# Tuned float32 transformer block: a new order of the first token tiles, the first column group's product in true float32, and a new entry to the second SwiGLU

## The chip, the cores and the metric

The kernel runs on one core of a Trainium2 chip, in one launch. The metric is the device time of that launch in microseconds (us); what counts is the median of several runs.

## The reference

One block on x of 1024 tokens by 1024 channels, all in float32: a SwiGLU of half weight, a mix of two attentions, and a second SwiGLU of half weight.

```python
def rms_norm(x, g):
    x32 = x.astype(jnp.float32)
    y = x32 * lax.rsqrt(jnp.mean(x32 * x32, axis=-1, keepdims=True) + EPS) * g.astype(jnp.float32)
    return y.astype(x.dtype)

def swiglu(h, w_in, w_out):
    gate, up = jnp.split(h @ w_in, 2, axis=-1)
    return (jax.nn.silu(gate) * up) @ w_out

def hybrid_layer(x, ...):
    x = x + 0.5 * swiglu(rms_norm(x, ffn1_norm), ffn1_w_in, ffn1_w_out)
    h = rms_norm(x, mix_norm)
    proj = h @ w_mix_in
...
    x = x + mix @ w_mix_out
    x = x + 0.5 * swiglu(rms_norm(x, ffn2_norm), ffn2_w_in, ffn2_w_out)
    return x
```

The inner width of a SwiGLU is 2816, that is 22 column groups of 128 for the gate and as many for the other half. The change touches only the start of each SwiGLU; the attention between them is left as it is.

## The kernel before

**Tiles and products.** The tokens lie in eight tiles of 128, `X[0]` to `X[7]`; in instruction names these are `x_74` to `x_81`, and the trace calls all of them `x`. Each tile has two halves of 512 channels (`HALF`). A tile is scaled by its inverse root mean square, transposed on TensorE (`flip4`, L312, four 128x128 float32 transposes for a half), and copied back from PSUM in place (L552 on VectorE, which multiplies by the norm's gain on the way where one is given; L557 on ScalarE where none is). Products need float32 accuracy and use the float32r type: both operands are split into a high part and a low part, and a product is three matmuls, high by high, low by high, high by low (`mm3`, L250 to L252). The high part of a transposed half comes from ScalarE (L540) or GpSimd (L545), the low part from VectorE (L320, `flip_lo`). Weights are split in the same way by `split` (high L456 or L458, low L461).

**The order.** All steps are entered into a list scheduler with `add(engine, cost, position, emit, deps, after, takes, tail)`; it writes out, for each engine, one fixed order by the costs and positions given. Engines run that order in sequence and wait on semaphores, so an instruction that waits holds up all behind it on its engine. Loads and stores are issued by SyncE, in the order of the list too.

**The start of a SwiGLU** (`first_stage`). The tokens are taken in two sets, tiles 0 to 3 and 4 to 7 (`half` 0 and 1), so that a product has 512 columns. The first two column groups (`plain=2`) are plain products, group 0 and group 1 for either set; the other groups save products by working on sums and differences of halves (`S1` to `S4`, made by L704). The four weight blocks of a group (two halves of channels, gate and other) are 256 KB each.

**At the start of the kernel** a tile's two halves are loaded one by one, squared on ScalarE (L501), and the inverse root is a square root on ScalarE (L507) with a Newton step on VectorE (L474 to L477); L1004 scales the tile, half of tiles 0 and 1 on VectorE and the rest on GpSimd, which also splits all four weight blocks of group 0 into high and low (L458, L461). TensorE runs `WARM` = 8 groups of three warm-up transposes first (L489). Group 0 for tiles 0 to 3 is computed in two pieces of 256 columns (`pieces`), all else in 512.

**At the end of the attention** the block's last products (`pvo`, L1889 and L1890, with the low parts `pl` from VectorE, L1880) are followed by the last output products (`mo`, L250 to L252). Between them tiles 0 to 3 enter the second SwiGLU: the gain of its norm is loaded into `Psel` (4 KB, to all partitions), L521 multiplies a tile by its inverse root and by the gain in one VectorE operation of 128x1024, tile 3 takes two GpSimd operations for each half (L2011, L2013); then come the transposes, the copy back on ScalarE, high parts on GpSimd and low parts on VectorE.

Of the kernel before, what the change touches and what calls it, by code (L numbers as in the profile page):

```python
# [8 lines left out]
F32 = mybir.dt.float32  # L9
# [10 lines left out]
NT = 8  # L20
D = 1024
# [167 lines left out]
def block_kernel(  # L189
# [248 lines left out]
    def fetch(src, pos, deps=(), k=4, tail=2.2, cost=0.75):  # L438

        b, us = {}, []  # L440

        def emit():
            b["r"] = ws.place()
            dma(b["r"].rearrange("p (k f) -> p k f", k=k) if k > 1 else b["r"], src)
        fetched.append(add("S", cost, pos, emit, deps=deps, after=fetched[-1:], takes=[(r_raw, us)], tail=tail))
        return b, fetched[-1], us
# [33 lines left out]
    def root(st, pos, dep, table=0.0):  # L480
        c = add("A", 0.1 + table, pos, lambda: ACT.activation(st["y"], st["v"], AF.Sqrt), deps=[dep])
# [55 lines left out]
    def split_half(place, dst, t, pos, deps, eng="A"):  # L537

        def high():
            (ACT.activation if eng == "A" else copy_pool)(dst()[0][:, :, t % 4 * 128:t % 4 * 128 + 128], place(), AF.Copy)  # L540
        hi = add(eng, 0.6, pos, high, deps=deps)
        return [hi, add("D", 0.69, pos, lambda: flip_lo(place(), dst(), t), deps=[hi])]

    def copy_pool(o, i, _):
        POOL.tensor_scalar(o, i, 1.0, 1.0, op0=OP.mult, op1=OP.mult)  # L545

    def flip_in_place(t, c, dst, pos, deps, free, gain=None):
# [3 lines left out]
        if gain:  # L551
            back = add("D", 0.69, pos, lambda: DVE.tensor_tensor(  # L552
                in_blocks(t, c), b["p"].rearrange("p (k t) -> p k t", k=4),
                gain(c).unsqueeze(2).to_broadcast([128, 4, 128]), op=OP.mult), deps=[p])
            au.append(back)
            return [back] + split_half(lambda: in_blocks(t, c), dst, t, pos, [back, *free])
        back = add("A", 0.6, pos, lambda: ACT.activation(  # L557
            in_blocks(t, c), b["p"].rearrange("p (k t) -> p k t", k=4), AF.Copy), deps=[p])
        au.append(back)
        return [back] + split_half(lambda: in_blocks(t, c), dst, t, pos, [back, *free], "G" if t < 4 else "A")  # L560
# [39 lines left out]
    def open_in(p, x):  # L600
# [1480 lines left out]
```

## Time and profile before

| | us |
|---|---|
| median of 3 runs | 1925.83 (1923.86 to 1927.3) |
| the profiled execution's own time | 1925.15 |
| its span in the trace | 1923.4 |
| TensorE busy | 1877.4 (98%) |
| VectorE busy | 1379.9 (72%) |
| ScalarE busy | 921.7 (48%) |
| GpSimd busy | 433.9 (23%) |

The span runs from the first to the last instruction of the profiled execution; its own time is 1.75 us longer, and the median of the runs lies 0.68 us above that. TensorE is busy nearly all the time, so a time can only be won where TensorE waits, or where it does less, or where its clock is low. In the profile's rows PE is TensorE, DVE VectorE, ACT ScalarE, POOL GpSimd, SP SyncE. "out<-in" names what an instruction writes and reads, x8 that eight of a kind are merged in a row, and brackets hold the idle time before a row and what ended it.

### The profile page before, as it was taken

Reading aid. Unit: us, or ns where it says so; the run is one execution under the profiler, and the core shown is the slowest. Engines: PE = TensorE matmul, PEld = TensorE weight load, DVE = VectorE, ACT = ScalarE, POOL = GpSimd, SP = SyncE. Lnnn points to the kernel's source line nnn. Section 1 sums busy time; section 2 is a strip of 40 time slices with the busy share of each in tenths; the row PEclk is TensorE's granted clock in tenths of the full one; section 3 lists DMA queues with packets and bytes.
Section 4 is the critical chain, followed back from the end, with each engine's and each line's share of the span. In section 5 each row is a group of like instructions: output and inputs, shape, how many; then the busy total and the mean of one; then the engine's idle time right before and its main releaser. Section 6 shows DMA issues by size and latency. Waiting matters only on the chain.

```text
span 1923.4 us, 27849 instructions
## 1 busy us (share of the span) xinstructions
PE 1877.4 (98%) x9014; PEld 1564.6 (81%) x9014; DVE 1379.9 (72%) x3119; ACT 921.7 (48%) x1955; POOL 433.9 (23%) x574
## 2 busy tenths in 40 slices
PE   7999999999999999998899999989999999999999
PEld 6788888888888888887788778777888888888887
DVE  7977876665655677567888888879878766655553
ACT  5433333334444444246877888745333333344442
POOL 5111111111000112014754765542111111110000
PEclk9999999999999999998999999999999999999999
DMA  5367753336986337244201321023676532368662
GB/s 170 103 229 237 233 187 100 99 121 224 310 274 190 103 97 193 66 133 157 67 19 61 97 69 56 23 77 98 230 241 227 189 104 91 128 226 307 192 217 99
DMA packets 244083, 290.76 MB, mean 151 GB/s; under 512 B 25169, under 2 KB 139233, under 8 KB 243937
## 3 DMA queue, kind: packets, MB, share of 16 engines
q1 hardware_dynamic: 243936, 288.98, 46.7%
q8 instruction: 71, 1.16, 0.3%
q14 instruction: 76, 0.61, 0.1%
HBM read 201.72 MB, written 90.33 MB: 152 GB/s over the span
## 4 chain that ended last, share of the span: by engine, by line
PE 92%; DVE 4%; ACT 2%; POOL 2%; issue 1%; DMA 1%; SPq 0%; DVEq 0%; ACTq 0%; POOLq 0%
PE lg L251 13%; PE lg L250 13%; PE lg L252 13%; PE mo L250 6%; PE mo L251 6%; PE mo L252 6%; PE pv L250 4%; PE pv L252 4%; PE pv L251 4%; PE ptr L1870 3%; PE a L250 3%; PE a L251 3%; PE a L252 3%; PE pvo L1890 2%; PE pvo L1889 2%; PE lg L1695 2%
## 5 line engine op out<-in xcount | busy, mean ns | idle before, releaser
L834 POOL TENSOR_TENSOR x<-x,x 128x512 f32<-128x512 f32 x80 | 116.5, 1456 | 684.6 <-DVE x L830 628.8
L461 DVE TENSOR_TENSOR wlo<-wraw,whi 128x512 fp32r<-128x512 f32 x286 | 207.7, 732 | 70.8 <-ACT whi L456 69.3
L456 ACT ACTIVATE whi<-wraw 128x512 fp32r<-128x512 f32 x274 | 170.3, 623 | 102.2 <-PE lg L251 46.0
L461 DVE TENSOR_TENSOR gpl<-graw,gph 128x512 fp32r<-128x512 f32 x154 | 106.8, 697 | 124.6 <-ACT gph L456 124.6
L456 ACT ACTIVATE gph<-graw 128x512 fp32r<-128x512 f32 x154 | 96.1, 629 | 190.6 <-PE pv L251 88.2
L826 ACT ACTIVATE x<-lg 128x512 f32<-128x512 f32 x96 | 57.4, 598 | 156.5 <-PE lg L252 156.4
L1880 DVE TENSOR_TENSOR pl<-ptr,ph 128x512 fp32r<-128x512 f32 x178 | 116.4, 684 | 17.4 <-ACT ph L1878 16.2
L1878 ACT ACTIVATE ph<-ptr 128x512 fp32r<-128x512 f32 x178 | 98.7, 595 | 33.1 <-PE ptr L1870 32.0
L88 POOL TENSOR_SCALAR whi<-wraw 128x512 fp32r<-128x512 f32 (+1 forms) x52 | 35.2, 681 | 320.1 <-PE mo L252 211.6
L456 ACT ACTIVATE whi<-x 128x512 fp32r<-128x512 f32 x108 | 67.4, 627 | 82.2 <-PE lg L251 41.6
L251 PE MATMUL lg<-xn0l,whi 128*128 128x512 f32 (+1 forms) x264 | 100.9, 382 | 3.3 <-DVE xn0l L320 3.3
L250 PE MATMUL lg<-xn0h,whi 128*128 128x512 f32 (+1 forms) x264 | 101.3, 384 | 3.0 <-ACT xn0h L540 1.5
L250 PE MATMUL a<-whi,gph 128*128 128x512 f32 x264 | 103.1, 391 | 0.0
L252 PE MATMUL a<-whi,gpl 128*128 128x512 f32 x264 | 102.8, 389 | 0.0
L251 PE MATMUL a<-wlo,gph 128*128 128x512 f32 x264 | 102.7, 389 | 0.0
L252 PE MATMUL lg<-xn0h,wlo 128*128 128x512 f32 (+1 forms) x264 | 100.5, 381 | 0.0
L461 DVE TENSOR_TENSOR wlo<-x,whi 128x512 fp32r<-128x512 f32 x108 | 73.7, 685 | 32.2 <-ACT whi L456 31.7
L830 DVE TENSOR_TENSOR x<-lg,x 128x512 f32<-128x512 f32 x72 | 49.7, 690 | 55.9 <-PE lg L252 55.4
L250 PE MATMUL lg<-whi,gph 128*128 128x512 f32 x198 | 77.0, 389 | 0.0
L252 PE MATMUL lg<-whi,gpl 128*128 128x512 f32 x198 | 77.0, 389 | 0.0
L251 PE MATMUL lg<-wlo,gph 128*128 128x512 f32 x198 | 77.0, 389 | 0.0
L1758 POOL TENSOR_SCALAR Psel<-Psel,sc,gates 128x256 f32<-128x256 f32 (+7 forms) x60 | 52.1, 871 | 45.8 <-DVE sc L1750 19.5
(518 smaller groups left out, 5684.6 us busy)
## 6 DMA issues: line engine op xcount, KB each, us to landing
wraw<-in_ffn_w_in_dram SPq DMA_DIRECT2D x176, 256.0 KB, 3.4
wraw<-in_ffn_w_out_dram SPq DMA_DIRECT2D x66, 256.0 KB, 3.3
x<-in_ffn_w_out_dram SPq DMA_DIRECT2D x44, 256.0 KB, 4.0
qd<-qst SPq DMA_DIRECT2D x32, 256.0 KB, 2.2
xn0l<-qd SPq DMA_DIRECT2D x32, 256.0 KB, 2.8
wraw<-in_w_mix_in_dram SPq DMA_DIRECT2D x28, 256.0 KB, 2.9
x<-in_x_dram SPq DMA_DIRECT2D x12, 512.0 KB, 7.8
side<-in_ffn_w_out_dram SPq DMA_DIRECT2D x22, 256.0 KB, 4.6
```

Of the source, the lines that this page charges most:

```text
L250: PE.matmul(o, ah, bh, start=first, stop=False, **kw)
L251: PE.matmul(o, ah, bl, start=False, stop=False, **kw)
L252: PE.matmul(o, al, bh, start=False, stop=last, **kw)
L456: ACT.activation(w["h"], b["r"], AF.Copy)
L461: low = add(low, 0.69 if low == "D" else 1.25, pos + 0.5, lambda e=DVE if low == "D" else POOL: e.tensor_tensor(w["l"], b["r"], w["h"].bit ...
L826: ACT.activation(b["r"], o["o"], act)
L830: return add("D", 0.69, at, lambda b=tb[k], o=bx[o]: DVE.tensor_tensor(b["r"], o["o"], b["r"], op=OP.add), deps=deps)
L834: return add("G", 1.25, at, lambda a=tb[a], b=tb[b]: POOL.tensor_tensor(a["r"], a["r"], b["r"], op=OP.mult), deps=deps)
L1758: POOL.tensor_scalar(P[:, off:e], P[:, off:e], sc, gate, op0=OP.mult, op1=OP.mult)
L1870: PE.transpose(p[:, h * 128:(h + 1) * 128], s.P[h][:, c:c + 128], ident)
L1878: ACT.activation(st["ph"], st["p"], AF.Copy)
L1880: lo = add("D", 0.6, pos + 0.2, lambda st=st: DVE.tensor_tensor(st["pl"], st["p"], st["ph"].bitcast(F32), op=OP.subtract), deps=[hi])
```

## The change

In the first SwiGLU:

1. Group 0 for tiles 0 to 3 is no longer made of split parts. `whole` multiplies the weights as loaded (`raw0`, float32) by the transposed tile in place (float32), one matmul of 128x128x128 for each of four blocks, two halves and two parts: 16 a tile, 64 in all, in place of 96 of 256 columns. `raw0` stands where the high part of `S2` comes later (`s2_place`).
2. The tiles come one by one: tile 0's transposes, its product, tile 1's transposes, its product, and so on. Inverse roots are made by `inv_rms_of`, for tiles 1 to 3 singly, for 4 and 5 and for 6 and 7 together. Scaling goes by halves (`scale_half`): VectorE and ScalarE for tiles 0 and 1, GpSimd for the rest.
3. The split of group 0 is due later, since only tiles 4 to 7 need it now; its low parts go to VectorE.
4. Tile 1's load waits for 1.7 us in the plan (`come(1.7)`), and the plan now puts two other loads ahead of it.
5. Group 0 for tiles 4 to 7 is computed in two pieces of 256 columns.

In the second SwiGLU: the gain is no longer loaded to all partitions and multiplied; `gcol2` holds it by channel, and the copy back multiplies it, on VectorE. Scaling goes by halves, ScalarE for the first half of tiles 0 to 3, GpSimd for all else. The transposes take first halves of tiles 0 to 3, then second halves; the second wait for tile 3's first (`fl["A11", 3]`). High parts go to ScalarE.

```diff
-    def scale_in_place(t, r, gain, pos, deps):
-        return add("D", 1.22, pos, lambda: DVE.scalar_tensor_tensor(
-            X[t], X[t], r(), gain(), op0=OP.mult, op1=OP.mult), deps=deps)
+    def scale_half(t, c, r, pos, deps, eng, **kw):
+        def emit():
+            x = X[t][:, HALF[c]]
+            if eng == "A":
+                ACT.activation(x, x, AF.Copy, scale=r())
+            elif eng == "D":
+                DVE.tensor_scalar(x, x, r(), None, op0=OP.mult)
+            else:
+                POOL.tensor_scalar(x, x, r(), 1.0, op0=OP.mult, op1=OP.mult)
+        return add(eng, {"A": 0.6, "D": 0.36, "G": 0.66}[eng], pos, emit, deps=deps, **kw)
+    def inv_rms_of(a, n, pos, deps):
...
+        for t in range(a, a + n):
+            for h in range(2):
+                sq.append(add("A", 0.75, pos, lambda t=t, h=h, first=not sq: (first and place(), square(t, h)), deps=deps[t - a],
+                              after=sq[-1:], takes=[] if sq else [(r_y, yu)]))
+        return st, root(st, pos, add("D", 0.4, pos, total, deps=sq), late=0.2)[1], yu
...
-            wait = fl["A11", 1] if begin and t < 2 and c else []
-            fl[name, q] = flip_in_place(t, c, lambda: opn()[name], at, deps + wait[-1:], free, gain)
+            wait = fl["A11", 3][-1:] if t < 4 and c and not begin else []
+            fl[name, q] = flip_in_place(t, c, lambda: opn()[name], at, deps + wait, free, gain, 6.0 if begin and t < 4 else 0.0)
...
+        def whole(o, raw, t, j):
+
+            x = in_blocks(t, j)
+            for a in range(4):
+                PE.matmul(o["o"][:, 128 * t:128 * t + 128], raw["r"][:, 128 * a:128 * a + 128], x[:, a], start=j == a == 0,
+                          stop=j == 1 and a == 3, skip_group_check=True)
...
-                    W[n, j, part] = split(b, t, us, pos - 4.0 + 8 * n, weigh, low="G" if begin and n == 0 else "D")
+                    W[n, j, part] = split(b, t, us, pos + (16.0, 6.0)[n] + 0.4 * j + 0.2 * part if begin else pos - 4.0 + 8 * n, weigh)
...
-                for c0, c1 in (pieces if n == half == 0 else [(0, 512)]):
+                for t, j, part in [(t, j, part) for t in range(4) for j in range(2) for part in range(2)] if begin and n == half == 0 else []:
...
+                    chain.append(add("P", 0.95, at, emit, deps=[arrived, here[0]], after=chain[-1:], takes=takes))
+                    at += 0.68
...
+                for c0, c1 in [] if begin and n == half == 0 else pieces if n == 0 else [(0, 512)]:
...
+            if begin and q == 0:
+                s2_open = [add(None, 0.0, at, begin, after=[u for j in range(2) for k in range(2) for u in raws[0, j, k][2]])]
+            parts_of("S2", q, t, 0, at + 2.0, [s2, opened], s2_open if begin else [])
...
-            fetched.append(add("S", 1.7, -20.0, lambda t=w_: load_x(t, n=2 if t < 4 else 1), after=fetched[-1:], tail=2.6))
+            fetched.append(add("S", 1.9, -20.0, lambda t=w_: load_x(t, n=2 if t < 4 else 1), after=fetched[-1:], tail=2.8,
+                               deps=[come(1.7)] if w_ == 1 else []))
...
-    gain2 = add("S", 1.5, tail, lambda: load_gain(nx["t"][:, 0, :D], ffn2_norm), deps=[nb], tail=2.2)
...
-        scaled[t] = scale_in_place(t, lambda t=t: R2[:, t:t + 1], lambda: nx["t"][:, 0, :D], p_, [put_, r_, gain2])
+        scaled[t] = [scale_half(t, c, lambda t=t: R2[:, t:t + 1], p_ + c, [put_, r_], "A" if t < 4 and c == 0 else "G") for c in range(2)]
```

How the order of instructions moves is shown at three places; `raw_401` is `raw0`.

TensorE at the kernel's start, before: after the warm-ups the first halves of tiles 0 and 1, then products of split parts (`xn0` from tiles, `whi` and `wlo` from weights) for both.

```order
L489 MATMUL warm<-ident 128x128 x24
L312 MATMUL ntr<-ident,x_74 128x128 x4
L312 MATMUL ntr<-ident,x_75 128x128 x4
L250 MATMUL lg<-xn0h,whi 128x256
L251 MATMUL lg<-xn0l,whi 128x256
L252 MATMUL lg<-xn0h,wlo 128x256
```

TensorE at the same place, changed, up to group 1's first product:

```order
L491 MATMUL warm<-ident 128x128 x24
L312 MATMUL ntr<-ident,x_74 128x128 x8
L671 MATMUL lg<-x_74,raw_401 128x128 x16
L312 MATMUL ntr<-ident,x_75 128x128 x8
L671 MATMUL lg<-x_75,raw_401 128x128 x12
L312 MATMUL ntr<-ident,x_76 128x128 x8
L671 MATMUL lg<-x_75,raw_401 128x128 x4
L312 MATMUL ntr<-ident,x_77 128x128 x8
L671 MATMUL lg<-x_76,raw_401 128x128 x16
L671 MATMUL lg<-x_77,raw_401 128x128 x16
L250 MATMUL pv<-xn0h,whi 128x512
```

The first product now needs tile 0 alone, and no split part of anything; the transposes of tiles 2 and 3 stand within the products of tiles 1 and 2.

SyncE's first loads, changed (before, tile 1 came right behind `gcol`, then two weight blocks, tile 2, two weight blocks, tile 3):

```order
L257 DMA x_74<-in_x_dram 128x512 x2
L257 DMA gcol<-in_ffn_norm_dram 128x2x4
L257 DMA side_402<-in_ffn_w_out_dram 128x512
L257 DMA side_403<-in_ffn_w_out_dram 128x512
L257 DMA x_75<-in_x_dram 128x512 x2
L257 DMA raw_401<-in_ffn_w_in_dram 128x4x128 x2
```

Two blocks of 256 KB of the output weights, which nobody needs yet, have come ahead of tile 1.

TensorE at the second SwiGLU's entry, changed:

```order
L1923 MATMUL ptr<-ident,Pwin 128x128 x4
L1942 MATMUL pvo<-ph,vwin 128x512
L1943 MATMUL pvo<-pl,vwin 128x512
L312 MATMUL ntr<-ident,x_74 128x128 x4
L1942 MATMUL pvo<-ph,vwin 128x512
L1943 MATMUL pvo<-pl,vwin 128x512
L312 MATMUL ntr<-ident,x_75 128x128 x4
L1942 MATMUL pvo<-ph,vwin 128x512
L1943 MATMUL pvo<-pl,vwin 128x512
L312 MATMUL ntr<-ident,x_76 128x128 x4
L312 MATMUL ntr<-ident,x_77 128x128 x4
L250 MATMUL mo<-whi,mh 128x512
```

Before, the last `pvo` and the first `mo` had 24 transposes between them (tiles 1, 2 and 3, both halves); now they have 8, and 12 more stand behind the six `mo` products, ahead of the first product of the second SwiGLU.

## Rows read from the trace of the kernel before

**Rows 1.** The page: the span, and section 1 for TensorE (busy, share, instructions).

```profile
span 1923.4 us, 27849 instructions
...
PE 1877.4 (98%) x9014; PEld 1564.6 (81%) x9014; DVE 1379.9 (72%) x3119; ACT 921.7 (48%) x1955; POOL 433.9 (23%) x574
```

**Rows 2.** Waits of TensorE, first 110 us: total, times, longest, in us.

```profile
PE lg L251 <- DVE xn0l L320: 2.3, 1, 2.3
PE lg L251 <- DVE xn1h L320: 1.9, 1, 1.9
PE lg L250 <- ACT xn1h L540: 1.7, 1, 1.7
PE lg L250 <- ACT xn0h L540: 1.5, 1, 1.5
```

**Rows 3.** Timeline of TensorE, 1.3:20: start, duration, instruction, [idle before <-releaser].

```profile
1.38 7.62 PE L489 MATMUL warm<-ident 128*128 128x128 f32 x24 [1.38 <-DVE ident L297]
13.19 1.99 PE L312 MATMUL ntr<-ident,x 128*128 128x128 f32 x8 [4.20 <-DVE x L1004]
```

**Rows 4.** Windows, 9:58: stretch, length, busy by engine, PEclk, DMA share, GB/s.

```profile
19.57:23.80 4.23, 4.23 (x20) 4.23 (x21) 1.35 (x6) 0.61 (x2) 3.69 (x7) 1.00 0.97 365
23.80:35.96 12.16, 12.16 (x102) 12.06 (x100) 10.67 (x28) 8.20 (x21) 0.54 (x2) 1.00 0.26 76
35.96:50.80 14.84, 14.84 (x82) 12.70 (x80) 14.56 (x27) 9.21 (x17) 11.51 (x12) 1.00 0.11 37
50.80:58.00 7.20, 3.58 (x9) 2.52 (x9) 7.20 (x9) 3.19 (x6) 4.52 (x4) 0.76 0.00 0
```

**Rows 5.** Timeline of TensorE, 50.3:59: products after the two waits.

```profile
55.69 0.63 PE L252 MATMUL lg<-xn1h,wlo 128*128 128x512 f32 x1
56.12 0.63 PE L250 MATMUL lg<-xn1h,whi 128*128 128x512 f32 x1
...
58.12 0.40 PE L252 MATMUL lg<-xn1h,wlo 128*128 128x512 f32 x1
58.35 0.39 PE L250 MATMUL lg<-xn1h,whi 128*128 128x512 f32 x1
```

**Rows 6.** Timeline of ScalarE, 0:24: squares of the first two halves that come.

```profile
3.68 0.63 ACT L501 ACTIVATE junk<-x 128x512 bf16<-128x512 f32 x1 [1.12 <-DMA x<-in_x_dram]
...
6.44 0.63 ACT L501 ACTIVATE junk<-x 128x512 bf16<-128x512 f32 x1 [2.04 <-DMA x<-in_x_dram]
```

**Rows 7.** Timeline of GpSimd, 0:24: fourth weight block of group 0.

```profile
13.12 0.88 POOL L458 TENSOR_SCALAR whi<-wraw 128x512 fp32r<-128x512 f32 x1 [0.26 <-DMA wraw<-in_ffn_w_in_dram]
```

**Rows 8.** Windows of 10 us: the second.

```profile
10.00:20.00 10.00, 2.97 (x11) 2.31 (x12) 8.90 (x22) 5.07 (x14) 9.15 (x10) 1.00 0.98 304
```

**Rows 9.** Timeline of TensorE, 783.2:786.5: float32 products, moving operand strided.

```profile
783.25 3.45 PE L1417 MATMUL cpre<-kc2k,cw 128*128 128x128 f32 x15
```

**Rows 10.** Timeline of TensorE, 817.6:818: float32 products, 64 columns in sequence.

```profile
817.65 0.55 PE L1449 MATMUL cout<-cw,chid 128*128 128x64 f32 x4
```

**Rows 11.** Waits of TensorE, 1230:1330, around the second SwiGLU's entry.

```profile
PE pvo L1890 <- DVE pl L1880: 2.6, 4, 1.2
PE mo L251 <- DVE xn2h L320: 1.7, 1, 1.7
PE lg L250 <- POOL xn0h L545: 1.4, 1, 1.4
PE lg L251 <- DVE xn0l L320: 1.0, 1, 1.0
...
PE ntr L312 <- DVE x L521: 0.4, 1, 0.4
```

**Rows 12.** Timeline of VectorE, 1255:1285: the scaling of one tile.

```profile
1263.54 1.69 DVE L521 SCALAR_TENSOR_TENSOR x<-x,rstd,Psel 128x1024 f32<-128x1024 f32 x1
```

**Rows 13.** Timeline of GpSimd, 1255:1285: one operation, twice.

```profile
1255.40 0.69 POOL L2011 TENSOR_SCALAR x<-x,rstd 128x512 f32<-128x512 f32 x1 [3.17 <-DVE rstd L477]
...
1260.27 1.67 POOL L2011 TENSOR_SCALAR x<-x,rstd 128x512 f32<-128x512 f32 x1
```

More of the change, by code (lines that the diff above doesn't have):

```diff
@@ L436, in conv, with fetch @@
         units[u] = (low, us)
-    def fetch(src, pos, deps=(), k=4, tail=2.2, cost=0.75):
-        b, us = {}, []
+    def fetch(src, pos, deps=(), k=4, tail=2.2, cost=0.75, at=None):
+        b, us = at or {}, []
         def emit():
-            b["r"] = ws.place()
+            if not at:
+                b["r"] = ws.place()
             dma(b["r"].rearrange("p (k f) -> p k f", k=k) if k > 1 else b["r"], src)
-        fetched.append(add("S", cost, pos, emit, deps=deps, after=fetched[-1:], takes=[(r_raw, us)], tail=tail))
+        fetched.append(add("S", cost, pos, emit, deps=deps, after=fetched[-1:],
+                           takes=[] if at else [(r_raw, us)], tail=tail))
         return b, fetched[-1], us
@@ L478, in newton, with root @@
         return emit
-    def root(st, pos, dep, table=0.0):
-        c = add("A", 0.1 + table, pos, lambda: ACT.activation(st["y"], st["v"], AF.Sqrt), deps=[dep])
+    def root(st, pos, dep, table=0.0, late=0.0):
+        c = add("A", 0.1 + table + late, pos, lambda: ACT.activation(st["y"], st["v"], AF.Sqrt), deps=[dep])
         last_root[0] = c
@@ L598, in in_src, with open_in @@
         return dram_ap(w_in, 512 * j * 2 * FF + part * FF + n * 128, [[4 * 2 * FF, 128], [2 * FF, 4], [1, 128]])
-    def open_in(p, x):
-        t = {k: [p.tile([128, 4, 512], F32R, name=k + s) for s in "hl"] for k in ("S2", "S1", "S3")}
+    def open_in(p, x, s2="hl"):
+        t = {k: [p.tile([128, 4, 512], F32R, name=k + s) for s in (s2 if k == "S2" else "hl")] for k in ("S2", "S1", "S3")}
         t["S4"], t["A22"] = ([v[:, 4 * a:4 * a + 4] for a in range(2)] for v in x)
@@ L974, in block_kernel @@
     f_op = ExitStack()
-    opn1 = open_in(pool("p_in", f_op), xn[1])
+    opn1 = open_in(pool("p_in", f_op), xn[1], "l")
+    f_raw = ExitStack()
+    raw0 = pool("p_raw0", f_raw).tile([128, 4, 512], F32, name="raw0")
     side1 = [p_nw.tile([128, 512], F32, name="side%d" % j) for j in range(2)]
@@ L988, in block_kernel @@
         if type(w_) is tuple:
[L989 to L991 removed]
+            b = {"r": raw0[:, 2 * w_[1] + w_[2]]} if w_[0] == 0 else None
+            raws1[w_] = fetch(in_src(ffn1_w_in, *w_), -20.0, cost=0.95, tail=2.8, at=b)
+        else:
+            fetched.append(add("S", 1.9, -20.0, lambda t=w_: load_x(t, n=2 if t < 4 else 1), after=fetched[-1:], tail=2.8,
+                               deps=[come(1.7)] if w_ == 1 else []))
             xt[w_] = [fetched[-1]]
@@ L1030, in block_kernel @@
     gq, gk = {}, {}
+    gcol2 = cst.tile([128, 2, 4], F32, name="gcol2")
     f_out = ExitStack()
@@ L2031, in to_ffn2 @@
         extra2.extend(p.tile([128, 512], F32, name="ext2%d" % j) for j in range(4))
-    settled = add(None, 0.0, tail + 10.0, to_ffn2, deps=attention, after=list(scaled.values()))
+    settled = add(None, 0.0, tail + 10.0, to_ffn2, deps=attention, after=[x for v in scaled.values() for x in v])
     tile_no[0] = 4
     at, chain_, stored_, gone = first_stage(1, ffn2_w_in, ffn2_w_out, lambda: opn2, scaled, lambda: extra2[:2],
-                                             lambda: extra2[2:], tail + 6.0, "G", [], [(0, 512)], settled, done, side_free=[settled], plain=2)
+                                             lambda: extra2[2:], tail + 6.0, "G", [], [(0, 512)], settled, done, gain=lambda c: gcol2[:, c], side_free=[settled])
     def to_out2():
```

97 lines of the change are left out of this document (49 added, 48 removed).

## The prediction

> **What bounds the kernel now.** The page comes first: TensorE is busy for 1877.4 of a span of 1923.4 us [rows 1], so only some 46 us are open to a change that leaves TensorE's work as it is. TensorE's list of waits is the second view, taken for the two places that the diff touches. In the first 110 us the waits beyond the warm-ups are one of 4.20 us for tile 0 to be scaled [rows 3], two of 1.5 and 2.3 us for split parts of the first tiles, and two of 1.7 and 1.9 us for the parts of tiles 4 to 7 [rows 2]. Around the second SwiGLU's entry they are 2.6 us on `pl`, 0.4 us on the transposes, and 1.7, 1.4 and 1.0 us on high and low parts [rows 11]. The third view, busy time by stretches, shows that between the two places of the start TensorE has no gap at all: 12.16 of 12.16 us and 14.84 of 14.84 us [rows 4]. So I follow TensorE from instruction to instruction at both places and leave the middle at nothing: its order is the same, and TensorE, never idle for the other engines' sake there, hides what they do; without that cover each of their operations of 0.7 us that comes late would be lost time.
>
> The clock belongs to this. The stretch from 19.57 to 23.80 holds 20 records in 4.23 us, 0.21 each; the next holds 102 in 12.16 us, 0.12 each [rows 4], for products of 256 columns and transposes alike. The clock column reads 1.00 in both, but by the spacing the first ran at the lower level (1.2 GHz) and the second at the higher (2.4 GHz); the rise came 4.2 us after TensorE had begun to run without a gap. After the waits at 51 to 55 us it is seen again: 0.43 us from one product of 512 columns to the next, later 0.23 [rows 5], with a granted clock of 0.76 over that stretch [rows 4].
>
> **The start, step by step.** Two prices are needed. A transpose at the higher clock is 0.12 us, at the lower 0.21. The new float32 matmul is seen in no row of this shape. The nearest rows are two. L1417's matmuls of 128 columns make two records each, 15 records in 3.45 us, which is about 0.22 a record with the last one's longer end taken off [rows 9]; but its moving operand is read with a stride, so this is the upper end. L1449's, two records each too, are 64 columns in sequence, 4 records in 0.55 us: 0.09 between starts, if the last ends 0.27 after its start [rows 10]. That is the lower end if the weights set the pace. The new one reads 128 columns in sequence; I take 0.12, the price of a float32 transpose of the same shape, which is nearer to L1449's. So 64 matmuls are 128 records of 0.12, 15.4 us, where before 96 of 256 columns took 96 x 0.12 = 11.5 us. By itself the new product is 3.9 us dearer. What it saves is waiting.
>
> - Warm-ups end at 9.00 (1.38 + 7.62) and the first transposes started at 13.19, because tile 0 queued behind tile 1 on ScalarE and VectorE [rows 3]: the second square to run, at 6.44, waited 2.04 us for a DMA of tile 1 [rows 6]. Now tile 0 goes alone: from 3.68 on two squares of 0.63 [rows 6], 0.2 behind each for its sum, and an estimated 2 us for root, Newton step and scaling: about 7.4. That lies under the warm-ups; their end sets the start. Eight transposes at the lower clock take 1.99 us [rows 3], to 11.0; the first half is copied back (0.7) at about 10.9.
> - Tile 0's product is 32 records. Without a gap from about 10.7 the clock rises at 14.9 by the 4.2 us above: 19 records at 0.21 and 13 at 0.12, to 16.5. Its last weight block landed before at 13.05 or so, where GpSimd took it up [rows 7]. Two blocks of 256 KB now come ahead of it; at 304 GB/s [rows 8] each is 0.86 us, so 14.8. It is asked for after 24 records, at 15.6. Just in time.
> - Tile 1 lands 1.7 us later too, at 8.2 instead of 6.44, and its root stands on ScalarE behind tile 0's high parts (12.3); scaled at about 15, before TensorE is free. I charge 0.9 us for its copy back, behind which the product waits. Tiles 1 to 3 are then 3 x (8 + 32) records of 0.12, 14.4 us. End of group 0: 16.5 + 0.9 + 14.4 = 31.8, before 35.96. **Gain 4.2.**
> - The next 14.84 us (group 1, transposes of tiles 4 to 7) stay, to 46.6.
> - There the two waits of 1.7 and 1.9 us [rows 2] were for the last of four tiles. In pieces of 256 the product begins with tiles 4 and 5, so I take both off: **3.6.** The low clock behind them goes as well, 7 products of 0.43 in place of 0.23 [rows 5]: **1.4.** The pieces cost 96 x 0.12 = 11.5 instead of 48 x 0.23 = 11.0: **-0.5.** `S2` opens only when `raw0` is free and its high part now queues on ScalarE; I take a new wait of **-1.0** there, nothing to 2.5 as ends.
>
> Sum of the start: 4.2 + 3.6 + 1.4 - 0.5 - 1.0 = **7.7 us**. GpSimd's low parts (four, gone to VectorE at 0.7 each) cost nothing, since group 0 needs them 30 us later; without that cover they would be 2.8 us.
>
> **The second entry.** L521, 1.69 us for one tile on VectorE [rows 12], stood ahead of `pl` twice; with it go TensorE's 2.6 us on `pl` and 0.4 on the transposes [rows 11]: **3.0.** In its place are halves on ScalarE and GpSimd and a copy back on VectorE of 0.7 for each half. The other three waits (1.7, 1.4, 1.0) I leave standing, with other names: the last output product now has 8 transposes ahead of it instead of 24, so some 2 us less cover for the chain that adds and splits `pvo`'s output; and 12 transposes now stand ahead of the first product, cover for its split parts. The ends: 0.5 if a wait of 2.5 on that chain is new, 5.5 if the parts' waits go too.
>
> GpSimd's price there is not settled by one row. L2011 took 0.69 us on 128x512, and 1.67 beside L521 [rows 13]. The Trainium skill, "SBUF — State Buffer" (SBUF: two separate sides), says that VectorE and GpSimd share a pair of ports as an exclusive lock, and that a VectorE operation with two operands in SBUF shuts out a GpSimd operation that reads SBUF. The two rows agree, 0.69 against 1.67. By that rule the low parts (`xn0l` from `x` and `xn0h`, both in SBUF, 0.7 us) would hold the addition and the low part of the output chain once each, 1.4 us on that path; the entry would give 1.6 and the time would be 1916.5.
>
> **Sum.** 7.7 + 3.0 = 10.7 us. The profiled execution took 1925.15, 1.75 above its span; 1925.15 - 10.7 = 1914.45. The median of the runs is 0.7 above that execution: **1915.1**.
>
> **Rivals.**
> - *The clock stays low longer.* Float32 records with copy-back gaps between tiles may not bring the rise: the rest of tile 0 and all of tile 1, 13 + 40 records, at 0.21 instead of 0.12, 5.0 us: 1920.1. For it: every gap at the start was followed by the lower level. Against: transposes, float32 as well, ran at 0.12 within the stretch from 23.80. Chance 0.12.
> - *The second entry gives nothing.* The waits on `pl` turn into one on the output chain, since GpSimd has up to twelve halves to scale around its two operations there and the cover is 16 transposes shorter: 1918.1. For it: [rows 13], and three waits on parts that stay. Against: scaling halves of tiles 4 to 7 is not urgent. Chance 0.13; with the clock rival together (1923.1) another 0.03.
> - *The float32 matmul costs as L1417's, 0.22 a record.* 128 x 0.098 = 12.5 us more turn the start's 7.7 into a loss of 4.8. With an entry that gives nothing the kernel is slower, 1930.6; with a good one, 1927.6. It decides from 0.18 a record on, where the start gives nothing. For it: the only row of the same shape. Against: L1449's spacing, and no reason but the stride for 0.22 there. Chance 0.06, half of it with a useless entry.
>
> **How the numbers follow.** The forecast has 0.66, from about 1911.5 (float32 records at 0.09, 128 x 0.03 = 3.8 less) to about 1917.5 (second entry at 0.5). The range goes on to the first two rivals, to 1921.5; it leaves out the dear matmul, the two rivals together and the tails. A measurement of this kernel can tell about 0.2%, 3.9 us, so the bound is 1921.9. Faster: forecast, clock, useless entry: 0.66 + 0.12 + 0.13 = 0.91. Within: the two together and the dear matmul with a good entry, 0.03 + 0.03 = 0.06. Slower: 0.03.
>
> **What would show it.** In the profile after: TensorE's first transposes at 9.0 and L671's first record near 11; its records 0.12 apart after 15; group 1 (`pv`) beginning near 31.8; no wait above 0.5 us near 46 to 51 and no low clock there; the first `S2` product some 7 to 8 us earlier than before. At the entry no VectorE operation of 1.69 us, no wait on `pl` above 0.3, and perhaps one at the first `mo`. It is wrong if L671's records stand 0.18 apart or more, if tile 1 keeps TensorE idle for over 2 us, or if a wait of more than 2 us appears before `mo` or the first `lg`.

## The result, and the profile after

| | us |
|---|---|
| changed kernel, median of 4 runs | 1911.3 (1910.23 to 1911.94) |
| kernel before, median of 4 runs beside them | 1925.05 (1923.86 to 1927.3) |
| ratio | 0.9927 (95% interval 0.9915 to 0.9939) |
| profiled execution of the changed kernel | 1910.23, span 1908.5 |

The change is faster by 13.75 us by the medians; the forecast was 10.7. The time lies 0.2 us under the lower end of the range, so the prediction was wrong, on the good side. The two profiled executions are 14.9 us apart in span (1923.4 and 1908.5), more than the medians, since the one of the changed kernel was the fastest of its four; the sums below go by this pair.

The head of the page and the first engine's row of section 1 (busy time, share, instructions) [answers to rows 1]:

```profile
span 1908.5 us, 27998 instructions
...
PE 1874.3 (98%) x9094; PEld 1565.7 (82%) x9094; DVE 1373.8 (72%) x3120; ACT 920.8 (48%) x1951; POOL 428.6 (22%) x568
```

TensorE is busy 3.1 us less than before, and the span is 14.9 us shorter, so 11.8 us of the gain is idle time. TensorE's list of waits over the first 110 us (engine, line, what was waited for, total, times, longest) [answers to rows 2]:

```profile
...
PE ntr L312 <- DVE x L528: 0.7, 1, 0.7
PE lg L671 <- DVE x L576: 0.5, 1, 0.5
```

All the waits of before are gone but the 1.4 us ahead of the first warm-up; two short ones stand ahead of tile 1. The timeline of TensorE there (start, duration, instruction, idle before it) [answers to rows 3]:

```profile
8.79 1.91 PE L312 MATMUL ntr<-ident,x 128*128 128x128 f32 x8
10.63 3.97 PE L671 MATMUL lg<-x,raw 128*128 128x128 f32 x32
15.28 1.24 PE L312 MATMUL ntr<-ident,x 128*128 128x128 f32 x8 [0.67 <-DVE x L528]
17.03 2.94 PE L671 MATMUL lg<-x,raw 128*128 128x128 f32 x24 [0.52 <-DVE x L576]
...
29.83 0.48 PE L250 MATMUL pv<-xn0h,whi 128*128 128x512 f32 x1
```

The 32 records of tile 0's product take 3.97 us, from the second on 0.11 apart: TensorE's clock is at its higher level in all but the first, where the prediction had 19 of 32 at the lower. (In other executions the rise came up to six records later, see below.) Group 1 begins at 29.83 instead of 35.96.

What the start gives in all is read where both kernels run the same products without a wait again: group 1's first product for tiles 4 to 7. Before, in the timeline of TensorE:

```profile
67.20 0.39 PE L250 MATMUL lg<-xn1h,whi 128*128 128x512 f32 x1
```

and changed:

```profile
56.27 0.40 PE L250 MATMUL lg<-xn1h,whi 128*128 128x512 f32 x1
```

That is 10.9 us. At the second SwiGLU's entry, the waits of the changed kernel from 1215 to 1320 us [answers to rows 11] are:

```profile
PE mo L250 <- ACT mh L1981: 2.2, 1, 2.2
PE mo L251 <- DVE xn2h L320: 1.9, 1, 1.9
PE mo L252 <- POOL ml L1983: 1.4, 1, 1.4
PE pvo L1943 <- DVE pl L1933: 0.7, 3, 0.3
...
PE mo L250 <- ACT xn2h L568: 0.5, 1, 0.5
```

The 2.6 us on `pl` have shrunk to 0.7, and the 1.4 and 1.0 us before the first product are gone; new are 2.2 us on `mh` and 1.4 us on `ml`, both on the chain behind the last attention product. Behind them the clock falls once (window, length, busy, clock, DMA):

```profile
1257.00:1261.00 4.00, 4.00 (x19) 0.60 0.01 4
```

### The profile page after: what moved, and what is told of

Same layout as the page of the kernel before. It is cut to its first block, busy times and chain, and to the rows that moved or that the text cites. A ratio compares the mean times of both kernels' runs of the same rounds, so it can differ in the third digit from the quotient of the medians.

```text
span 1908.5 us, 27998 instructions
## 1 busy us (share of the span) xinstructions
PE 1874.3 (98%) x9094; PEld 1565.7 (82%) x9094; DVE 1373.8 (72%) x3120; ACT 920.8 (48%) x1951; POOL 428.6 (22%) x568
## 4 chain that ended last, share of the span: by engine, by line
PE 92%; DVE 2%; ACT 2%; POOL 1%; issue 1%; DMA 1%; SPq 0%; DVEq 0%; ACTq 0%
PE lg L250 13%; PE lg L252 13%; PE lg L251 13%; PE mo L250 6%; PE mo L252 6%; PE mo L251 6%; PE pv L250 4%; PE pv L252 4%; PE pv L251 4%; PE ptr L1923 3%; PE a L252 3%; PE a L250 3%; PE a L251 3%; PE pvo L1943 2%; PE lg L1748 2%; PE pvo L1942 2%
## 5 line engine op out<-in xcount | busy, mean ns | idle before, releaser
L250 PE MATMUL lg<-xn0h,whi 128*128 128x512 f32 x232 | 90.7, 391 | 0.0
L252 PE MATMUL lg<-xn0h,wlo 128*128 128x512 f32 x232 | 90.3, 389 | 0.0
L251 PE MATMUL lg<-xn0l,whi 128*128 128x512 f32 x232 | 90.3, 389 | 0.0
```

The lines of the kernel that those rows point to most:

```text
L250: PE.matmul(o, ah, bh, start=first, stop=False, **kw)
L251: PE.matmul(o, ah, bl, start=False, stop=False, **kw)
L252: PE.matmul(o, al, bh, start=False, stop=last, **kw)
```

## The experiments

Twelve kernels ran, each beside runs of the kernel before on the same chip; medians of before in these sets lay between 1924.06 and 1925.45. "The changed kernel" is 1911.3 in all comparisons, from its own set; since the medians of before differ by up to 1.4 us between sets, a difference of one or two us between kernels of different sets is not certain.

### The two places apart

`start_alone` is the changed start with the old second entry, `entry_alone` the reverse. One line of each diff:

```diff
# start_alone
-        scaled[t] = [scale_half(t, c, lambda t=t: R2[:, t:t + 1], ...) for c in range(2)]
+        scaled[t] = scale_in_place(t, lambda t=t: R2[:, t:t + 1], lambda: nx["t"][:, 0, :D], p_, [put_, r_, gain2])
# entry_alone
-        scaled[t] = scale_in_place(t, lambda t=t: R2[:, t:t + 1], lambda: nx["t"][:, 0, :D], p_, [put_, r_, gain2])
+        scaled[t] = [scale_half(t, c, lambda t=t: R2[:, t:t + 1], ...) for c in range(2)]
```

> The changed start of the first SwiGLU with the old entry of the second. Theory (the start is worth more than forecast, because TensorE's clock is already high for tile 0's product; the two places add up): the start gives the 10.9 us that the traces show between the first instruction and the first S2 product, and the single wait of 1.46 us on the query transposes in the middle, that went too, belongs to the start's shift: 10.9 to 12.1 us under before, 1913.0 to 1914.2. Rival (what went in the middle belongs to the new entry, because its gain vector is now loaded in the middle): 10.9 at most, and the 1.46 us wait stays. Waits at the second entry as before: 2.6 us on pl, 1.4 and 1.0 on parts.

> The old start with the new entry of the second SwiGLU. Theory: 2.7 us under before (1922.3), the difference that the traces show between the last attention products and the second SwiGLU's products; waits on mh (2.2) and ml (1.4) before the output products, no wait on pl over 0.3. Rival (the entry gives nothing by itself, all comes from the start): within 1 us of before.

`start_alone` took 1913.47 us, ratio 0.994 (0.9928 to 0.9953), 12.0 us under before; `entry_alone` 1924.31, ratio 0.9995 (0.9986 to 1.0004), no change that can be told. So the start brings nearly all. The waits of `start_alone` from 1200 to 1330 us are the old ones:

```profile
PE pvo L1956 <- DVE pl L1946: 2.8, 5, 1.2
...
PE lg L250 <- POOL xn0h L578: 1.4, 1, 1.4
...
PE lg L251 <- DVE xn0l L320: 1.1, 1, 1.1
```

and those of `entry_alone` the new ones:

```profile
PE mo L250 <- ACT mh L1933: 2.2, 1, 2.2
PE mo L251 <- DVE xn2h L320: 1.9, 1, 1.9
PE mo L252 <- POOL ml L1935: 1.4, 1, 1.4
...
PE pvo L1895 <- DVE pl L1885: 1.1, 5, 0.3
```

The old list holds 2.8 + 1.4 + 1.1 = 5.3 us that the new one answers with 2.2 + 1.4 + 1.1 = 4.7, and the whole lists add up to 9.4 and 8.9: the new entry exchanges waits. By the pair of traces of before and after it is worth 2.7 us; by the medians of the changed kernel and `start_alone`, 2.2; alone, 1.1, inside the noise.

Why these differ, the traces show. Six kernels (the changed one, `entry_alone`, and four of the runs below: `no_come`, `half1_512`, `after_warm3`, `tile1_first`) run the same instructions in the same order from the last attention product (`pvo`) on, with the same four waits of 2.16, 1.36, 0.49 and 1.90 us, to 0.02. From the start of that product's last record to the end of the span they take 657.6 us (the changed kernel, `no_come`, `half1_512`), 659.0 (`after_warm3`), 660.1 (`tile1_first`) and 660.2 (`entry_alone`). What differs is the clock behind the waits: how long it stays low behind the one on `ml`, and whether it falls again behind the one on `xn2h`. Here are 6 us from that wait's end, in the changed kernel and in `tile1_first`:

```profile
1292.55:1298.55 6.00, 6.00 (x26) 1.00 0.00 0
1294.68:1300.68 6.00, 6.00 (x20) 0.75 0.00 0
```

So the 2.7 us of the pair hold a clock that was kind to the changed kernel: in the trace of `entry_alone`, 2.6 us longer from there on, next to nothing is left of them.

### What raised the clock

Two kernels put a gap ahead of tile 0's product. In `no_come` tile 1's load stands right behind tile 0's again; the clock was not the aim, but the new order lets tile 1's root steps stand ahead of tile 0's copy back on VectorE.

```diff
-                               deps=[come(1.7)] if w_ == 1 else []))
+                               deps=[]))
```

> The changed kernel, with tile 1's load right behind tile 0's again and the two blocks of output weights later. Theory: tile 1 lands some 1.5 us earlier and the weight blocks too, but tile 1's root stands on ScalarE behind tile 0's high parts whatever it lands, so the two gaps before tile 1 (0.67 and 0.52 us) stay and the time is that of the changed kernel within 0.5 us. Rival: the landing sets those gaps; they go, and with them about 1.2 us (1910.1).

It took 1912.28 us, ratio 0.9933 (0.9921 to 0.9946): the same as the changed kernel within the noise, but not for the reason that was expected. Its timeline of TensorE:

```profile
...
11.24 3.78 PE L671 MATMUL lg<-x,raw 128*128 128x128 f32 x16 [0.53 <-DVE x L576]
...
30.91 0.48 PE L250 MATMUL pv<-xn0h,whi 128*128 128x512 f32 x1
```

The gaps before tile 1 are gone, as the rival had it. In their place is one of 0.53 us before tile 0's product, and the 16 records behind it take 3.78 us, 0.21 apart, the lower clock. In the changed kernel the same product, without that gap, ran at 0.11 from its second record on. It is the same instruction on the same data, and up to the gap TensorE's records stand at the same times in both traces, to 0.01 us: the gap decides, not the kind of product. Group 1 begins at 30.91, 1.1 us later.

`after_warm3` makes a gap on purpose.

```diff
-WARM = 8
+WARM = 3
```

> The changed kernel with 3 groups of warm-up transposes in place of 8: TensorE stands still from about 4.3 us on until tile 0 is scaled (7.2) and again until the first weight block has come (9.3). Theory (what raised the clock for tile 0's product was TensorE running from 1.4 us on without a gap): tile 0's product, begun at about 9.4, runs 0.21 a record for four to five us, so it ends later than now (about 15 to 16 instead of 14.5) though it begins 1.2 sooner; group 1 begins 0.5 to 1.5 us later than now. Rival (float32 products bring the clock up at once): 0.11 a record from 9.4 on, held up by the fourth weight block at 13.1 and by tile 1 as now; group 1 at the same time.

1911.19 us, ratio 0.9933 (0.992 to 0.9947), again the same total.

```profile
...
9.51 5.39 PE L671 MATMUL lg<-x,raw 128*128 128x128 f32 x32 [0.60 <-DMA raw<-in_ffn_w_in_dram]
...
29.00 0.48 PE L250 MATMUL pv<-xn0h,whi 128*128 128x512 f32 x1
```

Tile 0's product begins at 9.51 and takes 5.39 us instead of 3.97: its first 15 records come 0.21 apart, the rest 0.11. So float32 products alone do not bring the clock up at once, and the theory holds on that. The rest of the expectation missed: the product ended 0.3 us later than that of the changed kernel (14.9 against 14.6), but group 1 began 0.8 us sooner, since most of the waiting for tile 1 fell away. Warm-ups that fill the time to tile 0 buy the clock for its product, and here that is paid back by the later beginning.

`before_warm14` asked the same of the kernel before.

```diff
-WARM = 8
+WARM = 14
```

> The kernel before with 14 groups of warm-up transposes in place of 8, which fill the 4.2 us in which TensorE waits for tile 0. Theory (the clock rises when TensorE has run without a gap, whatever it runs, at about 10.6 us after the start as in the changed kernel): the later warm-ups come 0.11 apart instead of 0.21 from about 10.6 on. What follows: if the short waits behind (1.5 and 2.3 us) let it fall again, the time stays as before; if not, the 20 records up to 23.8 come at 0.12 and 1.9 us are won (1923.5). Rival (the float32 product raised the clock in the changed kernel): all warm-ups and the first products at 0.21, time as before.

1925.05 us, ratio 1.0001 (0.9992 to 1.001). The scheduler did not put the added warm-ups into the gap as meant: ten groups ran to 10.9, a gap of 2.05 us stayed, and four groups came behind tile 0's transposes. All of them ran 0.21 apart within their groups, and so did the products to 25.3 us. It shows that warm-ups spread around gaps bring nothing; whether warm-ups alone would have raised the clock at 10.6 it leaves open.

How soon the clock rises without a gap also varies. Nine traces have the same records on TensorE up to tile 0's product, which begins at 10.63 or 10.64 without a gap. In four (the changed kernel, `start_alone`, `flips_free`, `tile1_first`) the spacing falls to 0.11 at the second or third record, and the 32 take 3.85 to 4.03 us. In the other five (`pool_clear`, `hold_clock`, `half1_512`, `best_a`, `best_b`) it falls only behind the sixth or seventh, and the 32, where they come in one row, take 4.48 to 4.64, as in `best_a`:

```profile
10.64 4.64 PE L676 MATMUL lg<-x,raw 128*128 128x128 f32 x32
```

So some 0.6 us of what the start gives differ from execution to execution. With the gap of `no_come`, 16 records and five transposes of tile 1 ran at 0.21, more than in any of the nine; that is one trace. Nor is the delay of the rise behind TensorE's last wait a fixed time: it was 4.2 us before, 3.3 in `after_warm3`, 4.6 in `no_come` and 5.9 in `before_warm14`.

### Pieces of 256 columns

```diff
-                for c0, c1 in [] if begin and n == half == 0 else pieces if n == 0 else [(0, 512)]:
+                for c0, c1 in [] if begin and n == half == 0 else [(0, 512)]:
```

> The changed kernel with group 0 for tiles 4 to 7 in one piece of 512 columns again. Theory: the first product then waits at 44.8 us for the parts of tiles 6 and 7, whose last low part is done near 46.6, two waits of some 0.8 and 0.9 us; the pieces' own extra of 0.5 us is saved; if the clock falls behind the waits, another 1.4: 1.2 to 2.6 us more than the changed kernel. Rival (the parts are early now in either form, because all ahead of them begins 6 us sooner): 0.5 us less than the changed kernel.

1913.54 us, ratio 0.9944 (0.993 to 0.9958), 2.2 us more than the changed kernel, inside the 1.2 to 2.6 of the theory. Its timeline of TensorE at group 0 for tiles 4 to 7:

```profile
45.65 0.50 PE L250 MATMUL lg<-xn1h,whi 128*128 128x512 f32 x1 [0.64 <-ACT xn1h L568]
46.79 0.50 PE L251 MATMUL lg<-xn1h,whi 128*128 128x512 f32 x1 [0.63 <-DVE xn1h L320]
47.12 0.40 PE L252 MATMUL lg<-xn1h,wlo 128*128 128x512 f32 x1
47.35 0.39 PE L250 MATMUL lg<-xn1h,whi 128*128 128x512 f32 x1
```

Two waits of 0.64 and 0.63 us, and behind them products 0.23 apart: the clock stayed high. From the beginning of group 1 to its first product for tiles 4 to 7 this trace has 27.6 us (29.92 to 57.56), the changed kernel's 26.4, so the pieces are worth 1.2 us there. Of the 4.9 us that the changed kernel wins at this place they are thus the smaller part; the waits of 1.7 and 1.9 us had already shrunk to 0.64 and 0.63, and the low clock behind them had gone, with the other edits. (In this kernel's profiled execution 2.3 us more were lost at a wait in the middle, of which below.)

### The second entry

`flips_free` takes away the wait of the second halves' transposes.

```diff
-            wait = fl["A11", 3][-1:] if t < 4 and c and not begin else []
+            wait = []
```

> The changed kernel without the wait of the second halves' transposes for tile 3's first half, so that 8 more transposes stand ahead of the first output product. Theory: they fill about 1 us of the 2.2 us wait on mh, but their copies back stand on VectorE ahead of the low parts, so a wait on low parts of about 1 us comes back before the first product of the second SwiGLU: within 1 us of the changed kernel. Rival: the wait on mh and the low clock behind it (1.7 us) go and nothing comes back, 2 to 3 us less than the changed kernel (1908.8).

1915.46 us, ratio 0.995 (0.9937 to 0.9964): 4.2 us more than the changed kernel, beyond both expectations.

```profile
PE lg L250 <- ACT xn0h L568: 2.4, 1, 2.4
...
PE mo L252 <- POOL ml L1983: 0.9, 1, 0.9
...
PE mo L250 <- ACT mh L1981: 0.5, 1, 0.5
PE lg L251 <- DVE xn0l L320: 0.5, 1, 0.5
```

The waits on `mh` and `ml` fell from 3.6 to 1.4 us as foreseen, and 2.9 us on high and low parts came, so the sum of waits is only 0.8 us larger. The traces are 2.9 us apart in span. Most of the rest goes with the clock, which in this kernel's windows is 0.54 from 1261 to 1264 and falls again behind the wait on `xn2h` (0.79 from 1292 to 1300), where the changed kernel's stays at 1.00; but that second fall came in `tile1_first` and `entry_alone` without this edit, so it need not be the edit's. All five runs (1913.15 to 1916.17) are slower than all four of the changed kernel. So the added wait in the diff earns its place: it keeps the first product's high parts from queuing behind the second halves.

`pool_clear` moves tile 6's scaling on GpSimd behind `ml`. In the changed kernel GpSimd's timeline there is (start, duration, instruction):

```profile
1250.18 2.69 POOL L530 TENSOR_SCALAR x<-x,rstd 128x512 f32<-128x512 f32 x4 [4.32 <-DVE rstd L479]
1252.93 0.73 POOL L1975 TENSOR_TENSOR opart<-opart,opart 128x256 f32<-128x256 f32 x1
1253.64 1.67 POOL L530 TENSOR_SCALAR x<-x,rstd 128x512 f32<-128x512 f32 x1
1255.28 1.15 POOL L1983 TENSOR_TENSOR ml<-opart,mh 128x256 fp32r<-128x256 f32 x1
```

```diff
-        scaled[t] = [scale_half(t, c, ..., "A" if t < 4 and c == 0 else "G") for c in range(2)]
+        scaled[t] = [scale_half(t, c, ..., "A" if t < 4 and c == 0 else "G",
+                                after=[list(mixes.values())[-1][-1][1]] if t == 6 else []) for c in range(2)]
```

> The changed kernel, with tile 6's scaling on GpSimd moved behind the low part ml of the last attention output. Theory: ml starts right behind mh, about 0.9 us earlier than now, and the wait of 1.36 us on it falls to about 0.5; the wait of 2.16 us on mh and the low clock behind stay, so about 0.9 us less than the changed kernel. Rival (the wait is set by ScalarE and VectorE, GpSimd's 1.67 us beside it is only what it looks like): no change.

1909.13 us (1908.52 to 1910.19), ratio 0.9916 (0.9903 to 0.993), 2.2 us under the changed kernel.

```profile
PE mo L250 <- ACT mh L1981: 2.2, 1, 2.2
...
PE mo L252 <- POOL ml L1983: 0.4, 1, 0.4
```

The wait on `ml` fell from 1.4 to 0.4 us, as expected: GpSimd's scaling of 1.67 us was what held it. The clock in the two stretches behind the entry:

```profile
1257.00:1261.00 4.00, 4.00 (x25) 1.00 0.02 4
...
1292.00:1300.00 8.00, 8.00 (x30) 0.79 0.00 0
```

It does not fall at 1257 any more, but it falls later, behind the wait on `xn2h` (0.79 over 8 us). From the last attention product to the end this trace is 0.9 us shorter than that of the changed kernel (656.7 against 657.6). As a whole it is hardly shorter (1908.4 against 1908.5), because the part ahead of that product was 0.9 us longer, 0.5 of it in tile 0's product.

`hold_clock` fills the wait on `mh` with transposes of no use (for this, `warm_up` also takes a bank's name, and `flipped` keeps the transposes to wait for).

```diff
+        if not begin:
+            add("P", 2.0, pos, lambda: warm_up(18, "lg"), deps=[flipped[3, 0]], takes=[(r_lg, [])])
```

> The changed kernel with 18 more transposes of the identity in the wait of 2.16 us ahead of the last output products, to no use but to keep TensorE running. Theory: the clock falls at 1256.5 because TensorE stood still for most of 1252 to 1256.5; with only the wait of 1.36 us on ml left it stays high, the 17 records after it take 1.9 instead of 3.9 us, so 1.7 us or so less than the changed kernel. Rival: the 1.36 us alone bring it down: the same time within 0.3 us.

1910.59 us, ratio 0.992 (0.9907 to 0.9934): 0.7 us under the changed kernel, within the spread of the runs.

```profile
1252.00:1254.40 2.40, 2.40 (x24) 1.00 0.00 0
1254.40:1257.00 2.60, 1.32 (x8) 1.00 0.00 0
1257.00:1261.00 4.00, 3.71 (x15) 0.61 0.02 4
```

TensorE is busy all of 1252 to 1254.4, and the clock falls all the same (0.61), behind 1.36 us on `ml` alone. In this trace the rival was right; since equal waits brought unequal falls in the six traces above, one trace does not settle it for all executions.

### The start once more, and the best version

`tile1_first` queues tile 0's split parts behind tile 1's scaling.

```diff
-        return [back] + split_half(lambda: in_blocks(t, c), dst, t, pos + later, [back, *free])
+        return [back] + split_half(lambda: in_blocks(t, c), dst, t, pos + later, [back, *free], order)
```

(`order` is `scaled[1]` for tile 0 of the first SwiGLU, else empty.)

> The changed kernel, with tile 0's split parts queued behind tile 1's scaling on ScalarE and VectorE. Theory: tile 1's transposes then wait for nothing (0.67 us before), its copy back waits for less (0.52 before), group 1 begins about 1 us earlier, 28.8 instead of 29.83, and all behind it: 1 us less than the changed kernel. Rival: tile 0's late split parts hold group 1's first product, and the second is won nowhere: the same time.

1911.57 us, ratio 0.993 (0.9918 to 0.9943): the same. Its waits in the first 110 us:

```profile
PE lg L672 <- DVE x L576: 1.3, 1, 1.3
PE ntr L312 <- DVE x L528: 0.2, 1, 0.2
```

The transposes wait 0.5 us less and the product behind them 0.8 us more, since a low part of the weights took VectorE's free place, tile 0's own low part of 1.10 us came behind it, and the copy back began only at 16.46 us (16.30 in the changed kernel). The rival named the outcome, not this cause.

`best_a` joins the two edits of `pool_clear` and `hold_clock` with pieces of 256 columns for group 0 of tiles 4 to 7 in the second SwiGLU too; `best_b` adds to it the edit of `tile1_first` and puts the low parts of group 0's weights behind tile 1's copy back.

```diff
# best_a
-                                             ..., gain=lambda c: gcol2[:, c], side_free=[settled])
+                                             ..., gain=lambda c: gcol2[:, c], late=[(0, 256), (256, 512)], side_free=[settled])
...
-                for c0, c1 in [] if begin and n == half == 0 else pieces if n == 0 else [(0, 512)]:
+                for c0, c1 in [] if begin and n == half == 0 else late or pieces if n == 0 and half else pieces if n == 0 else [(0, 512)]:
# best_b, besides
+                    W[0, j, part][1].after.append(fl["A12", 1][0])
```

> The changed kernel with three edits at the second SwiGLU's entry: tile 6's scaling behind ml on GpSimd, the 18 idle transposes ahead of the last output products, and group 0 for tiles 4 to 7 in pieces of 256 there too. Theory: of the waits 2.2 (filled), 1.4 and 2.4 us only about 0.4 and 0.5 are left, no stretch at the lower clock in 1250 to 1300, the pieces cost 0.5: 1.0 + 1.9 - 0.5 and 1.7 for the clock, 4 us less than the changed kernel, 1907.2. Rival (the waits come back one product later): 1909, as with tile 6's scaling moved alone.

> As the one before, and at the start tile 0's split parts behind tile 1's scaling and the low parts of group 0's weights behind tile 1's copy back, so that tile 1's transposes stand within tile 0's product and nothing on VectorE ahead of its copy back. Theory: the two gaps at tile 1 (0.67 and 0.52 us) go, 1 us less than the one before. Rival (as in the earlier run with the split parts alone: another wait takes their place): the same as the one before.

`best_a` took 1905.31 us (1905.02 to 1907.29), ratio 0.9904 (0.9891 to 0.9918): 6.0 us under the changed kernel (5.0 if each is taken against the runs of before in its own set), the fastest of all that ran. Its windows:

```profile
1257.00:1261.00 4.00, 3.64 (x22) 1.00 0.02 4
...
1292.00:1300.00 8.00, 8.00 (x69) 1.00 0.01 2
```

No stretch at the lower clock is left behind the entry, and TensorE has no gap from 1292 to 1300, where the wait on `xn2h` was. From the last attention product to the end the trace has 652.8 us, 4.8 less than the changed kernel. What the pieces of 256 give there by themselves no run tells. `best_b` took 1910.06, ratio 0.9924 (0.9911 to 0.9938): tile 1's two gaps are gone as foreseen, but two other waits came.

```profile
PE lg L251 <- DVE xn1h L320: 1.9, 1, 1.9
...
PE ntr L312 <- POOL x L530: 0.9, 1, 0.9
```

Tile 3's scaling now stands behind weights on GpSimd, and a low part of tiles 4 to 7 comes 1.9 us late, with 16 products at 0.21 behind it; that the low parts which VectorE was made to put off are the reason was not tested. The gaps at tile 1 are cheaper than what it takes to close them in this way.

### The wait in the middle

The pair of traces of before and after also differs by 1.2 us (1.46 and 0.29) at one place in the mix projection, where TensorE waits for a VectorE root behind a weight load (`qtr`), before and after:

```profile
PE qtr L1132 <- DVE hr L474: 1.5, 1, 1.5
PE qtr L1185 <- DVE hr L476: 0.3, 1, 0.3
```

The expectation of `start_alone` gave it to the start; there it was 1.4 us still, and 0.2 in `entry_alone`, which looks like the rival. But it is neither. `best_a`, `hold_clock` and the changed kernel run the same instructions in the same order on every engine up to the second entry, and in `best_a` the wait is back:

```profile
PE qtr L1190 <- DVE hr L476: 1.6, 1, 1.6
```

Over all traces of this case it was 1.4 us or more in seven and 0.3 or less in seven. VectorE's own wait ahead of it is for the landing of a weight block, 0.63 us in the changed kernel, 1.15 before and 1.29 in `best_a`; but `start_alone` has 0.23 there and still waits 1.4 on `qtr`, so the landing alone does not decide it. What does, no run tells.

## Why the prediction was wrong, and where it was right

By its own steps, with what the pair of traces shows:

| step | predicted | measured |
|---|---|---|
| end of group 0 (group 1 begins) | 4.2 | 6.1 (35.96 to 29.83) |
| group 0 for tiles 4 to 7: waits, clock, pieces | 3.6 + 1.4 - 0.5 = 4.5 | 4.9 |
| a wait at `S2` | -1.0 | 0 |
| start | 7.7 | 10.9 |
| middle | 0 | 1.2, by chance |
| second entry | 3.0 | 2.7, in other traces of the same entry down to 0.1 |
| sum | 10.7 | 14.8 of 14.9 |

- **The step that failed** is tile 0's product: "19 records at 0.21 and 13 at 0.12, to 16.5". Measured are 32 records in 3.97 us, to 14.6: 1.9 us, all of what the term for group 0 missed. I let the count for the rise begin anew at 10.7, where the product was to begin behind a copy back, and gave the warm-ups nothing. In fact tile 0's transposes followed the warm-ups and the product followed the transposes without a gap, and the clock was up at the product's second record. Some 0.6 us of the 1.9 is luck of this execution: in five of nine traces the clock came with the seventh or eighth record. `no_come` and `after_warm3` show the step much as it was predicted, once a gap of 0.53 or 0.60 us stands ahead of the product: 16 and 15 records at 0.21. The count of 4.2 us itself came from one row and is no constant (3.3 to 5.9 us in four traces).
- The clock had a rival to the slow side only. The range's lower end, 1911.5, rested on the price of the float32 record alone, and by its own figures that end is 1915.1 - 3.8 = 1911.3; a clock that rises sooner had no place in it. The 0.2 us by which 1911.3 fell outside is less than the spread of the four runs (1.7); the 3.0 by which the medians' gain exceeds the forecast is not.
- **The wait at `S2`** for which 1.0 us was charged did not come: TensorE has no wait on it at all in the first 110 us. With the step above it makes up most of the miss.
- **The middle** was left at nothing because TensorE was taken to be never idle for the other engines there. Between 110 and 1230 us the trace of before has waits of 20.2 us in all, the one on `qtr` among them, which moved by 1.2 us.
- **The price of the float32 record** was right: 0.12 taken, 0.11 measured for 128 columns in sequence, two records a matmul. The Trainium skill, "FP8 and Floating Point Precision" (TensorE Precision Notes), gives true float32 four passes through the array, an estimate of 0.21 us for 128 columns at 2.4 GHz; the two records' 0.22 agree. Of the rival by which they cost 0.22 each, as L1417's with its stride, nothing is left.
- **The gaps ahead of tile 1** were charged with 0.9 us and measured 0.67 + 0.52.
- **The place at tiles 4 to 7** was right in size and partly wrong in cause: the pieces are worth 1.2 us of it (`half1_512`), not the whole 3.6; the rest went with the earlier parts.
- **The second entry** came near in size (3.0 against 2.7) by luck: two errors, and a clock that in other traces of the same entry takes back up to 2.6 us. The waits on parts, which I left standing, went (2.5 us); the waits on the output chain, which the text had named as an end of the range, came (3.5 us), one of them the wait of more than 2 us before `mo` that the text had named as a sign of being wrong; a stretch at the lower clock went. The scaling that the changed kernel has beside VectorE's low parts took 1.67 us, against 0.67 a piece (2.69 for four) beside copies back, which read PSUM, and `pool_clear` shows that this one operation held `ml` for 1.0 us. The Trainium skill, "SBUF — State Buffer" (SBUF: two separate sides), says that a VectorE operation with two operands in SBUF shuts out a GpSimd one that reads SBUF; these rows agree. The 1.4 us which the prediction worked out by that rule were for the addition and the low part themselves, and these took 0.73 and 1.15 us; that the wait on `ml` measured 1.36 is chance.
- **The rivals.** The clock went the other way, the dear float32 matmul is out, and the one on the second entry came nearest: the waits moved to the output chain as it said, and alone the new entry is inside the noise.

## What to carry to other kernels

Where work is made ready earlier, ask for every gap whether it leaves TensorE without work, and whether the clock is up by then: a product that followed the warm-ups without a gap came to the higher clock after one to seven records, and a gap of half a microsecond ahead of it brought 16 records at twice the price. Put such a gain into the range as well as the loss. Do not price a wait from one trace: six kernels with the same waits at the second entry differ by 2.6 us behind them, by the clock, while the two that have no wait over 0.4 us there (`best_a`, `best_b`) show no low stretch at all. Before an edit adds work to an engine, look at what stands ahead of the one operation that TensorE waits for: one scaling of 1.67 us on GpSimd, which nobody needed yet, held TensorE for 1.0 us.

## What the runs showed of the hardware that was not expected

- A gap's length alone does not tell whether the clock falls. Two waits of 0.64 and 0.63 us left it high (`half1_512`), and so did one of 1.3 ahead of tile 1's product (`tile1_first`); one of 1.36 us behind full work brought it down (`hold_clock`), and one of 2.2 us with 0.36 behind it did not at once (`pool_clear`, 1.00 from 1257 to 1261). Even the same waits behind the same work did not always bring the same fall (six traces, at the second entry). What decides between these is not settled here.
- The clock column reads 1.00 at the start of the kernel, while the records of one kind stand 0.21 apart in one kernel and 0.11 in the other; there the level is read from the spacing.
- Float32 matmuls straight from the weights, two records of 0.11 us for 128 columns, stand against three of float32r, 0.12 for 256 columns: 0.22 against 0.18 us per 128 columns and block, and no split to wait for.
